# Order of transposes, weight loads and weight sums in the MLP block products of a two-layer decoder trunk

## The chip, the cores and the metric

One core of one Trainium2 chip runs the whole kernel in one launch. The metric is the time of one execution on the device, in microseconds (us). TensorE (PE in the profile; its weight loads are PEld) multiplies, VectorE (DVE), ScalarE (ACT) and GpSimd (POOL) do the elementwise work, and SyncE (SP) issues most of the loads from the chip's memory. Each engine works through a queue of its own; semaphores connect them.

## The reference, cut to what matters

A trunk of two layers over 256 tokens of width 2048. Each layer is a mixer (a recurrent one in layer 0, an attention in layer 1), a residual add, a norm, and then an MLP with a hidden width of 8192:

```python
def squared_relu_mlp(h, w1, w2):
    return jnp.square(jax.nn.relu(h @ w1)) @ w2
...
        h = h + squared_relu_mlp(rms_norm(h, norm_mlp[layer]), mlp_w1[layer], mlp_w2[layer])
```

All inputs and weights are float32. The change concerns the two MLPs, which take about two thirds of the time.

## The kernel before, in words

**Float32 from a faster type.** A weight tile of 128 x 2048 float32 numbers (1 MB) is loaded by SP and then split: ScalarE casts it into `hi` (L102, the type fp32r), and VectorE subtracts, `lo = w - hi` (L103). Activations are kept as such pairs too (`bufa`, `bufb`, `formx`, `formh`). Each product is three matmuls: high by high, high by low, low by high. One 1 MB tile holds four contraction blocks of 128 by 512 columns, so a use of it with one token half is 4 x 3 = 12 matmuls of 512 columns.

**Blocks.** An MLP is done in four quarters `q` of the hidden width. A quarter has four blocks of four 512-column groups taken two by two: `first` for n0 = 0 and 2 (w1, result into `bufb` and `formh`), then `second` for n0 = 0 and 2 (w2, result added to `xres`, which the profile calls `xall`). So there are 32 blocks in the kernel: 2 layers x 4 quarters x 4. A block covers 1024 columns (two groups, n = 0 and 1) and both token halves (j = 0 and 1). Half of its contraction goes by a scheme of seven products instead of eight, on sums of weights and sums of activations; the other half is plain. `blocks` runs over eleven steps, the *units*, in the order of `ORDERS`; `i0 + k` below is the number of the weight tile:

| step | weight it multiplies | matmuls |
| --- | --- | --- |
| a | tile 0 | 12 |
| t1 | tile 0 + tile 4 | 12 |
| n | tile 6 (w1) or 7 (w2), plain, both token halves | 24 |
| t2 | tile 0 + 4 + 5 | 12 |
| c | tile 5 | 12 |
| n | tile 7 (w1) or 6 (w2), plain | 24 |
| t3 | tile 4 + tile 5 | 12 |
| d | tile 1 | 12 |
| n | tile 2, plain (called n2 below) | 24 |
| t4 | tile 0 + 4 + 5 + 1 | 12 |
| n | tile 3, plain (called n3 below) | 24 |

The steps called n6 and n7 are the plain ones with tiles 6 and 7. All TensorE instructions of `mm` (L176) and `turn` (L179) are chained by hand in program order; the other engines' orders are set by the scheduler, which follows the program's order and two priorities: `stream()` for loads, sums and splits, and `urgent()` for what empties the accumulators.

**Weights.** `fetch` runs two units ahead of the multiplication and calls `combine` for a block's unit. Raw tiles come from the pool `wraw`, a ring of three buffers (tile name `raw`), and each split goes into rings of three `hi` and three `lo` buffers. So the split of a unit waits until TensorE has finished the unit three before it. The tiles `a` and `t1` are different: each has one buffer in the pool `pair` (the profile calls `t1` `t`). `a` is loaded there, split for step a, and then changed in place: at step t1 VectorE adds `t1` to it (L142), at step t2 it adds the raw tile 5, and at step t4, in w2, the raw tile 1. In w1 that last sum is made by a load that GpSimd issues and that adds in memory (L138). Tile 5 is added to `t1` by such a load in both (L136). In every step with a sum, VectorE's sum stands right ahead of the cast and the subtraction that split its result:

```python
        if add:
            V.tensor_tensor(r, r, held[add], OP.add)
        made[u] = Weights(r)
```

**Results and transposes.** `events` empties an accumulator after a product: in `first`, `hold` copies it (L710), and `final` combines it with such a copy on VectorE (L736); `relu2` then takes relu (L714) and square (L715) on ScalarE. When both token halves of a 512-column group are done, `to_h` appends a piece of work to the list `later`: eight transposes on TensorE into `pl` (L179), a cast (L690) and a subtraction (L691) into `bufb`, and for n < 2 also a copy (L694), four combinations (L592 to L595) and their splits (L588, L589) into `formh`. `flush` runs the list. In `blocks` it is called at the end of every plain step, after `final` of that step:

```python
            for j in (1, 0) if n else (0, 1):
                times(sums[n, j], w, lambda i, j=j, g=g: plain(j, 4 * g + i))
                if plains[n] == 2:
                    final(n, j, sums[n, j])
            flush()
```

In `second`, `to_x` (L745) adds the results to `xres`, and in the last quarter `done` appends `to_features`, the transposes for the next layer.

Of the kernel before, what the change touches and what calls it, by code (L numbers as in the profile page):

```python
# [10 lines left out]
F32 = mybir.dt.float32  # L11
# [5 lines left out]
OP = mybir.AluOpType  # L17
# [3 lines left out]
P = 128  # L21
# [20 lines left out]
def trunk_kernel(ctx, tc, x, xtok, cols, tab, masks, pos, fin, w_in, w_gate, w_out, w_qkv, w_o, w1, w2, out):  # L42
    nc = tc.nc
# [3 lines left out]
    wraw = pool("wraw", 3)  # L47
# [9 lines left out]
    V, A, T = nc.vector, nc.scalar, nc.tensor  # L57
# [7 lines left out]
    units = []  # L65
    made = {}
# [10 lines left out]
    for step in ORDER.split():  # L77
        src, first, n = where[step[0]]
# [29 lines left out]
    def fetch():  # L108
        u = at[0]
        if u >= len(units):  # L110
            return
        at[0] += 1
        src, i = units[u][:2]
        with stream():
            if len(units[u]) > 2:
                combine(u, *units[u])
                return
            r = wraw.tile([P, 2048], F32, name="raw")
            nc.sync.dma_start(r, src[i])
            made[u] = Weights(r, 1024)  # L120

    held = {}

    def combine(u, src, i, what, i0):
        if what in ("a", "t1"):
            r = held[what] = pair.tile([P, 2048], F32, name=what)
            nc.sync.dma_start(r, src[i])
        elif i is not None:
            r = wraw.tile([P, 2048], F32, name="raw")
            nc.sync.dma_start(r, src[i])  # L130
            held[what] = r
        to, add = {"t1": ("a", "t1"), "t2": ("a", "t2"), "t3": ("t1", "t2"), "t4": ("a", "d"),
                   "a": ("a", None), "c": ("t2", None), "d": ("d", None), "n": ("n", None)}[what]
        r = held[to]
        if what == "t2":
            nc.gpsimd.dma_start(held["t1"], src[i], accum_op=OP.add)  # L136
        if what == "c" and src in T4_DMA(w1, w2):
            nc.gpsimd.dma_start(held["a"], src[i0 + 1], accum_op=OP.add)  # L138
        if what == "t3" or what == "t4" and src in T4_DMA(w1, w2):
            add = None  # L140
        if add:
            V.tensor_tensor(r, r, held[add], OP.add)  # L142
        made[u] = Weights(r)

    def fetch_first():
        for u in range(4):
# [18 lines left out]
    def unit(src, i):  # L165
        u = at[1]
        assert units[u][0] is src and units[u][1] in (None, i), (u, i)
        at[1] += 1
        if u + 2 >= at[0]:
            fetch()  # L170
        return made.pop(u)
# [3 lines left out]
    def mm(*args, **kw):  # L175
        chain[:] = [after(T.matmul(*args, **kw), chain)]  # L176
# [3 lines left out]

    later = []

    def flush():
        todo = later[:]
        later.clear()
        for f in todo:
            f()

# [66 lines left out]
    class FirstNorm:  # L255
# [3 lines left out]
        def add(self, blk):  # L259
            self.n += 1  # L260
            q = wk.tile([P, S], F32, name="t1", bufs=2)
            A.activation(q, blk, AF.Square)
            if self.n == 1:
                self.ss.append(wk.tile([P, S], F32, name="q", bufs=1))
                V.tensor_copy(self.ss[0], q)
            elif self.n < KB:
                V.tensor_tensor(self.ss[0], self.ss[0], q, OP.add)
            else:
                self.ss.append(q)
# [49 lines left out]
    def tokens(src, i0, mov, kgs=(0, 1, 2, 3), by_k=False):  # L319
        ks = PAIRED if src is w2 else range(KB)  # L320
        ps = [pmm.tile([P, 512], F32, name="p") for _ in range(2)]
        for g in kgs:
            w = unit(src, i0 + g)
            order = [(j, i) for i in range(4) for j in range(2)] if by_k else \
                [(j, i) for j in range(2) for i in range(4)]
            for j, i in order:
                k = ks[4 * g + i]
                h, l = w.part(i * 512, 512)
                xh = mov[:, k, j * P:j * P + P]
                xl = mov[:, k, S + j * P:S + j * P + P]  # L330
                first, last = g == kgs[0] and i == 0, g == kgs[-1] and i == 3
                mm(ps[j], xh, h, start=first, stop=False)
                mm(ps[j], xh, l, start=False, stop=False)
                mm(ps[j], xl, h, start=False, stop=last)
            flush()
        return ps
# [9 lines left out]
    def project(src, i, mov, acc=None):  # L346
        w = unit(src, i)
        p = pmm.tile([P, 512], F32, name="p")
        jobs = [(k, mov[:, k], k == 0, k == KB - 1) for k in range(KB)]
        if later:  # L350
            cross(p, w, jobs[:8], "h")
            flush()
            cross(p, w, jobs[8:12], "h")
            cross(p, w, jobs[:12], "l")
            jobs = jobs[12:]
        (acc or cross)(p, w, jobs)
        return p
# [211 lines left out]
    for step in ORDER.split():  # L569
        i = int(step[1])  # L570
# [72 lines left out]
    def blocks(src, i0, n0, mov, forms, events, final):  # L643
        plain = lambda j, k: (mov[:, k, j * P:j * P + P], mov[:, k, S + j * P:S + j * P + P])
        form = lambda f, k: (forms[:, k, 0, f * P:f * P + P], forms[:, k, 1, f * P:f * P + P])
        side = {"a": lambda i: plain(0, 2 * i), "d": lambda i: plain(0, 2 * i + 1), "t4": lambda i: plain(1, 2 * i + 1),
                "t1": lambda i: form(3, i), "t2": lambda i: form(0, i), "t3": lambda i: form(1, i),
                "c": lambda i: form(2, i)}
        alpha, delta, gamma = (pmm.tile([P, 512], F32, name="p") for _ in range(3))
        beta = psc.tile([P, 512], F32, name="po" if n0 else "pd", bufs=1)  # L650
        bank = {"a": beta, "t1": alpha, "t2": beta, "c": alpha, "t3": beta, "d": gamma, "t4": beta}
        sums = {(0, 0): gamma, (0, 1): beta, (1, 0): alpha, (1, 1): delta}
        opened = []

        def times(bank, w, get):
            for i in range(4):
                h, l = w.part(i * 512, 512)
                xh, xl = get(i)
                mm(bank, xh, h, start=not any(b is bank for b in opened), stop=False, skip_group_check=True)
                opened.append(bank)  # L660
                mm(bank, xh, l, start=False, stop=False, skip_group_check=True)
                mm(bank, xl, h, start=False, stop=i == 3, skip_group_check=True)

        plains = [0, 0]
        for what, u in ORDERS[src is w2]:
            w = unit(src, None if u is None else i0 + 4 * n0 + u)
            if what != "n":
                times(bank[what], w, side[what])
                if what in events:
                    events[what](bank[what])  # L670
                continue
            n, g = divmod(u, 4)
            plains[n] += 1
            for j in (1, 0) if n else (0, 1):
                times(sums[n, j], w, lambda i, j=j, g=g: plain(j, 4 * g + i))
                if plains[n] == 2:
                    final(n, j, sums[n, j])
            flush()

    def to_h(n, tiles):  # L680
        def work():
# [21 lines left out]
    def first(i0, n0):  # L703
# [23 lines left out]
        def final(n, j, bank):  # L727
            with urgent():
# [5 lines left out]
                else:  # L734
                    y = keep["y2" if n else "y1"]
                    V.tensor_tensor(y, bank, y, OP.subtract if n else OP.add)  # L736
                    relu2(n, j, y, y)

        blocks(w1, i0, n0, bufa, formx, {"a": hold("y1", 2), "t1": hold("y4"), "t2": hold("y2"), "t3": u3}, final)

    def second(i0, n0, nrm, r2, r2n, done, gains):
        def to_x(bank, j, n, r, last):
            at = slice(n * 512, n * 512 + 512)
            with urgent():
                V.scalar_tensor_tensor(xres[:, j, at], bank, r[:, j:j + 1], xres[:, j, at], op0=OP.mult, op1=OP.add)  # L745
                if nrm and last:
                    nrm.add(j, n)

        def u2(bank):
            to_x(bank, 0, n0 + 1, r2n, False)  # L750
            if gains:
                gains()

        def u3(bank):
            to_x(bank, 1, n0 + 1, r2n, True)
            done(n0 + 1)

        blocks(w2, i0, n0, bufb, formh,
               {"a": lambda b: to_x(b, 0, n0, r2, False), "t1": lambda b: to_x(b, 1, n0 + 1, r2, False),
                "t2": u2, "t3": u3},  # L760
               lambda n, j, b: to_x(b, j, n0 + n, r2, (n, j) != (1, 1)))
        done(n0)
# [144 lines left out]
    with urgent():  # L907
        for j in range(2):
            m = tmp.tile([P, 1], F32, name="fm", bufs=2)
            r = tmp.tile([P, 1], F32, name="fr", bufs=2)  # L910
# [5 lines left out]
            i = V.scalar_tensor_tensor(m, ss[:, LAST:LAST + 1], 1.0 / D, m, op0=OP.mult, op1=OP.add)  # L916
            sums2.append(getattr(i, "ins", i).name)
            i = A.activation(t, m, AF.Sqrt)
# [6 lines left out]
        for j in range(2):  # L925
            for n, e in ((0, A), (LAST, V), (1, A if j else V), (3, V if j else A)):
# [4 lines left out]
                elif e is A:  # L931
                    i = A.activation(x_, x_, AF.Copy, scale=rr[j])
                    if n == 3:
                        after(i, roots[1:])
                else:
                    i = V.tensor_scalar(x_, x_, rr[j], None, op0=OP.mult)
# [19 lines left out]
T4_DMA = lambda w1, w2: (w1,)  # L956
# [104 lines left out]
```

## Time and profile before

Three runs took 2359.38, 2362.19 and 2363.51 us; the median is 2362.19 us.

| what | value |
| --- | --- |
| the profiled execution: time | 2363.19 us |
| its span, first to last instruction | 2361.0 us |
| mean granted TensorE clock | 0.971 |
| PE busy | 2201.3 us (93%), 11044 matmuls |
| PEld busy | 1864.1 us (79%) |
| DVE busy | 1788.7 us (76%) |
| ACT busy | 1265.5 us (54%) |
| POOL busy | 44.6 us (2%) |
| read from memory | 460.78 MB, 196 GB/s over the span |
| loads of `a` / `t1` by SP, 32 each: median to landing | 5.0 / 6.1 us |
| loads of `raw` for w1 and w2 by SP, 192: median to landing | 5.3 us |
| adding loads by GpSimd into `t1` (32) / `a` (16): median to landing | 7.8 / 8.5 us |

Busy shares are means over stages with different limits, and a matmul's end is modelled, so a busy PE is not a PE at its best rate. A row of a timeline gives start, duration, engine, line, operation, output and inputs, and in brackets the idle time before it with what ended it. A row of waits gives who waited for whom, the sum, the number and the longest in us. In windows, the columns are start and end, length, busy time of each engine with its number of instructions, the granted clock, the share of the DMA engines, and GB/s.

### The profile page before, as it was taken

The page shows a single profiled execution, that of the slowest core. Times are in us where ns is not written, and L with a number is a line of the kernel's source. Part 1 is how long each engine was busy: PE and PEld are TensorE (multiplying, and loading weights), DVE is VectorE, ACT ScalarE, POOL GpSimd, SP SyncE. Part 2 cuts the span into 40 slices and gives each one's busy share as a digit, 9 for nine tenths or more (in the row PEclk, how much of TensorE's full clock was granted, in tenths as well). Part 3 has the DMA queues.
Part 4 walks back from the last instruction along what each step waited for, and adds up shares of the span by engine and source line. Part 5 has one row for each costly group of instructions (what it writes and reads, how often), then busy time and mean ns, then how long its engine had stood idle before and what let it go on. Part 6 is the DMA issues. An engine that isn't in the chain of part 4 may idle for free.

```text
span 2361.0 us, 27739 instructions
## 1 busy us (share of the span) xinstructions
PE 2201.3 (93%) x11044; PEld 1864.1 (79%) x11044; DVE 1788.7 (76%) x2078; ACT 1265.5 (54%) x1429; POOL 44.6 (2%) x57
## 2 busy tenths in 40 slices
PE   9999999989989988989999999998998999899897
PEld 8999998767777777767788888887776777677776
DVE  7767786777777777777877878567777786777777
ACT  6444675564554565455554444556545545545644
POOL 0000000000000000000000000000000000000000
PEclk9999999989999999999999999999999999999999
DMA  8444465665765666665664554656667567566763
GB/s 306 150 164 156 143 219 191 196 198 176 249 219 173 196 213 214 214 214 178 199 212 161 179 179 161 214 170 202 217 214 214 178 221 242 179 191 212 237 216 107
DMA packets 65857, 464.68 MB, mean 197 GB/s; under 512 B 7344, under 2 KB 8112, under 8 KB 10304
## 3 DMA queue, kind: packets, MB, share of 16 engines
q1 hardware_dynamic: 58176, 410.89, 47.9%
q0 software_dynamic: 7264, 51.42, 11.6%
q8 instruction: 87, 1.43, 0.2%
q10 hardware_dynamic: 288, 0.61, 0.1%
q14 instruction: 42, 0.34, 0.0%
HBM read 460.78 MB, written 2.10 MB: 196 GB/s over the span
## 4 chain that ended last, share of the span: by engine, by line
PE 59%; DVE 16%; ACT 11%; DMA 7%; issue 6%; ACTq 0%; SPq 0%; DVEq 0%
PE p L176 47%; DVE lo L103 9%; ACT hi L102 9%; DMA a<-in_w 6%; DVE a L142 4%; PE pd L176 4%; PE po L176 4%; PE pl L179 2%; DMA raw<-in_w 1%; PE pl L471 1%; ACT y L714 1%; ACT y L715 1%; DVE xall L745 1%; DVE y L723 0%; DMA xall<-in_x 0%
## 5 line engine op out<-in xcount | busy, mean ns | idle before, releaser
L103 DVE TENSOR_TENSOR lo<-raw,hi 128x1024 fp32r<-128x1024 f32 (+2 forms) x454 | 748.4, 1667 | 195.5 <-ACT hi L102 178.5
L102 ACT CAST hi<-raw 128x1024 fp32r<-128x1024 f32 (+2 forms) x454 | 626.9, 1408 | 441.9 <-PE p L176 379.0
L176 PE MATMUL p<-hi,bufb 128*128 128x512 f32 x1408 | 448.3, 391 | 0.3
L103 DVE TENSOR_TENSOR lo<-a,hi 128x2048 fp32r<-128x2048 f32 x128 | 293.0, 2289 | 181.8 <-ACT hi L102 181.8
L102 ACT CAST hi<-a 128x2048 fp32r<-128x2048 f32 x128 | 244.3, 1908 | 328.8 <-DVE a L142 199.2
L176 PE MATMUL p<-hi,bufa 128*128 128x512 f32 x1280 | 411.0, 392 | 3.5 <-DVE bufa L231 2.7
L176 PE MATMUL p<-bufa,hi 128*128 128x256 f32 (+1 forms) x1792 | 364.9, 317 | 0.1
L176 PEld LDWEIGHTS p<-hi,bufb 128*128 128x128 f32 x1408 | 264.7, 188 | 57.0 <-DVE xall L745 2.4
L176 PEld LDWEIGHTS p<-bufa,hi 128*128 128x128 f32 x1792 | 294.5, 190 | 18.9 <-DVE hz L413 0.3
L176 PEld LDWEIGHTS p<-hi,bufa 128*128 128x128 f32 x1280 | 241.0, 188 | 54.8 <-DVE bufa L231 3.6
L176 PE MATMUL p<-lo,bufb 128*128 128x512 f32 x704 | 275.7, 392 | 6.2 <-DVE lo L103 6.2
L176 PE MATMUL p<-bufa,lo 128*128 128x256 f32 x1152 | 255.5, 287 | 0.0
L176 PE MATMUL p<-lo,bufa 128*128 128x512 f32 x640 | 251.1, 392 | 1.0 <-DVE lo L103 1.0
L176 PEld LDWEIGHTS p<-bufa,lo 128*128 128x128 f32 x1152 | 189.3, 191 | 2.7
L176 PEld LDWEIGHTS p<-lo,bufb 128*128 128x128 f32 x704 | 132.3, 188 | 37.5 <-DVE lo L103 10.8
L179 PE MATMUL pl<-tab__181,y 128*128 128x128 f32 x256 | 48.1, 350 | 106.4 <-ACT y L715 106.4
L176 PEld LDWEIGHTS p<-lo,bufa 128*128 128x128 f32 x640 | 120.6, 188 | 27.0 <-DVE lo L103 2.6
L179 PEld LDWEIGHTS pl<-tab__181,y 128*128 128x128 f32 x256 | 40.1, 182 | 115.2 <-ACT y L715 113.1
L142 DVE TENSOR_TENSOR a<-a,raw 128x2048 f32<-128x2048 f32 x48 | 109.6, 2283 | 0.0
L176 PE MATMUL po<-hi,bufa 128*128 128x512 f32 x256 | 94.4, 432 | 0.0
L176 PE MATMUL pd<-hi,bufb 128*128 128x512 f32 x256 | 91.7, 425 | 0.0
L176 PE MATMUL p<-hi,formh 128*128 128x512 f32 x256 | 87.2, 402 | 1.8 <-ACT hi L102 1.8
(281 smaller groups left out, 2891.7 us busy)
## 6 DMA issues: line engine op xcount, KB each, us to landing
raw<-in_w SPq DMA_DIRECT2D x192, 1024.0 KB, 5.3
raw<-in_w_qkv SPq DMA_DIRECT2D x48, 1024.0 KB, 4.8
raw<-in_w_in SPq DMA_DIRECT2D x46, 1024.0 KB, 4.9
a<-in_w SPq DMA_DIRECT2D x32, 1024.0 KB, 5.0
t<-in_w SPq DMA_DIRECT2D x32, 1024.0 KB, 6.1
t<-in_w POOLq DMA_DIRECT2D x32, 1024.0 KB, 7.8
raw<-in_w_out SPq DMA_DIRECT2D x16, 1024.0 KB, 4.9
a<-in_w POOLq DMA_DIRECT2D x16, 1024.0 KB, 8.5
```

The costliest lines, as they stand in the source:

```text
L102: A.copy(h, w)
L103: V.tensor_tensor(l, w, h.bitcast(F32), OP.subtract)
L142: V.tensor_tensor(r, r, held[add], OP.add)
L176: chain[:] = [after(T.matmul(*args, **kw), chain)]
L179: chain[:] = [after(T.transpose(out_, in_, ident), chain)]
L471: T.matmul(pl[:, j], kq[:, js], halves(qp[:, js], c, True), start=True, stop=True)
L714: A.activation(y, src, AF.Relu)
L715: A.activation(y, y, AF.Square)
L745: V.scalar_tensor_tensor(xres[:, j, at], bank, r[:, j:j + 1], xres[:, j, at], op0=OP.mult, op1=OP.add)
```

## The change

Three things are changed, all in the MLP blocks.

- `flush` takes a number `due`. `blocks` notes the length of `later` before the products of a plain step and runs only so many pieces after them, so what `final` appends in this step is run after the next plain step. What t3 of a block appends is run after n2 as before; what n3's `final` appends is run after the first plain step of the next block.
- Tile 0 (`a`) is loaded into the ring `wraw` instead of the pool `pair`. A new tile `s` in `pair` holds the sums, and the first one is written as `s = a + t1` instead of in place. The ring then takes seven tiles of a block instead of six.
- Each sum on VectorE is issued one step earlier: `a + t1` ahead of the split of a, the sum with tile 5 (and the load of tile 5 and GpSimd's adding load into `t1`) ahead of the split of the plain step before t2, and in w2 the sum with tile 1 ahead of the split of n2. In w1 GpSimd's adding load into the sum is issued after the split of c instead of ahead of it.

```diff
     def combine(u, src, i, what, i0):
-        if what in ("a", "t1"):
-            r = held[what] = pair.tile([P, 2048], F32, name=what)
-            nc.sync.dma_start(r, src[i])
-        elif i is not None:
-            r = wraw.tile([P, 2048], F32, name="raw")
-            nc.sync.dma_start(r, src[i])
-            held[what] = r
-        to, add = {"t1": ("a", "t1"), "t2": ("a", "t2"), "t3": ("t1", "t2"), "t4": ("a", "d"),
-                   "a": ("a", None), "c": ("t2", None), "d": ("d", None), "n": ("n", None)}[what]
-        r = held[to]
-        if what == "t2":
-            nc.gpsimd.dma_start(held["t1"], src[i], accum_op=OP.add)
+        def load(name, j, home=wraw):
+            held[name] = home.tile([P, 2048], F32, name="raw" if home is wraw else name)
+            nc.sync.dma_start(held[name], src[j])
+
+        def add(to, x, y):
+            V.tensor_tensor(held[to], held[x], held[y], OP.add)
+
+        if what == "a":
+            load("t1", i0 + 4, pair)
+            load("a", i)
+            held["s"] = pair.tile([P, 2048], F32, name="s")
+            add("s", "a", "t1")
+        elif what in ("n", "d"):
+            load(what, i)
+        ahead = units[u + 1][2:3] if u + 1 < len(units) else ()
+        if ahead == ("t2",):
+            load("c", i0 + 5)
+            nc.gpsimd.dma_start(held["t1"], src[i0 + 5], accum_op=OP.add)
+            add("s", "s", "c")
+        if ahead == ("t4",) and src not in T4_DMA(w1, w2):
+            add("s", "s", "d")
+        made[u] = Weights(held[{"t1": "s", "t2": "s", "t3": "t1", "t4": "s"}.get(what, what)])
         if what == "c" and src in T4_DMA(w1, w2):
-            nc.gpsimd.dma_start(held["a"], src[i0 + 1], accum_op=OP.add)
-        if what == "t3" or what == "t4" and src in T4_DMA(w1, w2):
-            add = None
-        if add:
-            V.tensor_tensor(r, r, held[add], OP.add)
-        made[u] = Weights(r)
+            nc.gpsimd.dma_start(held["s"], src[i0 + 1], accum_op=OP.add)
...
-    def flush():
-        todo = later[:]
-        later.clear()
+    def flush(due=None):
+        todo = later[:due]
+        del later[:due]
         for f in todo:
             f()
...
             plains[n] += 1
+            due = len(later)
             for j in (1, 0) if n else (0, 1):
                 times(sums[n, j], w, lambda i, j=j, g=g: plain(j, 4 * g + i))
                 if plains[n] == 2:
                     final(n, j, sums[n, j])
-            flush()
+            flush(due)
```

## The prediction

> **What bounds the kernel now.** I read the page's chain first, then TensorE's waits, then windows cut at the block borders, then the timeline of one border.
>
> ```profile
> PE 59%; DVE 16%; ACT 11%; DMA 7%; issue 6%; ACTq 0%; SPq 0%; DVEq 0%
> PE p L176 47%; DVE lo L103 9%; ACT hi L102 9%; DMA a<-in_w 6%; DVE a L142 4%; PE pd L176 4%; PE po L176 4%; PE pl L179 2%; DMA raw<-in_w 1%; PE pl L471 1%; ACT y L714 1%; ACT y L715 1%; DVE xall L745 1%; DVE y L723 0%; DMA xall<-in_x 0%
> ```
>
> TensorE carries 59%, but the load of `a`, the sums into `a` (L142) and the splits (L102, L103) sit on the chain too: at times weights come late. What TensorE itself waited for:
>
> ```profile
> PE pl L179 <- ACT y L715: 106.4, 16, 9.4
> PE p L176 <- DVE lo L103: 31.4, 24, 2.4
> PE p L176 <- ACT hi L102: 3.6, 6, 1.0
> ```
>
> Sixteen waits, 6.65 us each, stand before the transposes of `to_h`: one for each of the 16 `first` blocks. The windows of one quarter's four blocks (two `first`, two `second`; columns: length, busy TensorE, weight load, VectorE, ScalarE, GpSimd, then clock):
>
> ```profile
> 618.49:672.54 54.05, 44.12 (x197) 35.90 (x196) 42.01 (x28) 33.41 (x30) 2.59 (x3) 0.96 0.73 218
> 672.54:722.40 49.86, 44.77 (x199) 37.00 (x197) 37.46 (x30) 30.43 (x30) 1.73 (x2) 0.94 0.65 207
> 722.40:765.05 42.65, 42.65 (x182) 35.17 (x181) 30.57 (x21) 17.95 (x11) 0.00 (x0) 0.96 0.55 198
> 765.05:811.30 46.25, 43.05 (x181) 34.69 (x180) 37.56 (x23) 20.82 (x11) 0.86 (x1) 0.96 0.63 205
> ...
> sum 192.81, PE 174.59 PEld 142.76 DVE 147.60 ACT 102.60 POOL 5.18; mean PE 43.65 PEld 35.69 DVE 36.90 ACT 25.65 POOL 1.30
> ```
>
> The same arithmetic takes 42.65 us in one block and 54.05 in another. The end of the longest, on ScalarE and then on TensorE:
>
> ```profile
> 657.22 1.91 ACT L102 CAST hi<-a 128x2048 fp32r<-128x2048 f32 x1 [1.78 <-DMA a<-in_w]
> 659.03 0.57 ACT L694 COPY y<-pl 128x512 f32<-128x512 f32 x1
> 664.08 1.90 ACT L102 CAST hi<-a 128x2048 fp32r<-128x2048 f32 x1 [4.47 <-DVE a L142]
> 665.88 0.59 ACT L714 ACTIVATE y<-pd 128x512 f32<-128x512 f32 x1
> ...
> 669.72 1.15 ACT L715 ACTIVATE y<-y 128x512 f32<-128x512 f32 x2
> ```
> ```profile
> 662.54 0.39 PE L176 MATMUL pd<-hi,bufa 128*128 128x512 f32 x1
> 670.92 1.97 PE L179 MATMUL pl<-tab__181,y 128*128 128x128 f32 x8 [7.99 <-ACT y L715]
> ```
>
> TensorE finishes n3 at 662.9. The relu of that very block cannot start, because ScalarE's queue is held at the cast of the summed weight, which waits 4.47 us for the sum, which waited for the late `a`. So the last square ends at 670.9, then come the transposes. After such a gap the clock is halved for a while (first line right after the gap that ended at 477.96, second 20 us later):
>
> ```profile
> 478.00:482.00 4.00, 4.00 (x14) 3.51 (x15) 4.00 (x5) 1.17 (x2) 0.00 (x0) 0.50 0.83 291
> 500.00:504.00 4.00, 4.00 (x19) 3.30 (x19) 2.81 (x3) 0.48 (x2) 0.00 (x0) 1.00 1.00 406
> ```
>
> **The loss to be won.** The blocks span 426.5 to 1198.4 and 1581.1 to 2351.0: 771.9 + 769.9 = 1541.8 us. A block is 180 matmuls; undisturbed, 36 start in 8.16 us (chain pieces), 0.2267 us each, so 32 blocks need 1305.6. The 32 `to_h` take 0.79 us of TensorE each when warm (653.72 to 654.51), 25.3; five groups of feature transposes inside the stage, 4.0. Floor 1334.9; loss 206.9. It divides so: before the late transposes 106.4 idle; behind them the half clock, 1.62 instead of 0.79 us for the transposes and on average 1.50 us more than 10.88 for the next block's first 48 matmuls (sixteen borders), 16 x 2.33 = 37.3; the rest, 63.2, is late weights: 39.3 of listed idle time in some 40 waits, 23.9 of slower matmuls behind them and unlisted starts.
>
> One rule bears on the 37.3. The Trainium skill, page "TensorE: Matmul & The Clock Gate", section "What's actually happening", has the array fall to half clock after an idle window of about 3.4 us and recover after a busy one; by it, as an estimate, sixteen recoveries cost at least 16 x 1.7 = 27 us, so the gain would be some 10 us smaller, 2191 in the end; the trace's 0.50 agrees with the half clock, and its 37.3 decides.
>
> **The change, part by part.**
>
> *Transposes one step later.* `due` is taken before `final`, so only `to_h` of n3 moves: from the end of its block behind the first `n` product of the next one, 2.72 + 2.72 + 5.44 = 10.9 us of matmuls later. Eight transposes, two casts (0.59), two subtractions (0.68), and for half of them a copy, four combinations (0.42) and two split pairs (0.6 + 0.69) move with them. The square ended 8.0 us behind n3 at worst here (9.4 the longest wait), so it lies inside the 10.9 even if nothing else improved. Removed: 106.4 + 37.3 = 143.7. The user that could now be late is the `second` block with n0=0: its n7, then t2 and c (2 x 2.72 us), then n6, which reads the columns of the last `to_h`. Transposes end 0.8 us behind n7; two casts behind one weight cast (1.91) and two subtractions behind one sum and one split (2.28 + 2.29) end about 5.3 us behind them. That matches the 5.4 us to its use: at most 1 us in one block of four, 8 us over all.
>
> *`a` through the ring.* `a` had one buffer, read until the split of t4; the load left at 650.82, landed 6.4 us later, and the split followed at 657.22. Now `a` takes the slot of `d`, free when d is split, some 9 us earlier, so it lands before n3 is split. It hides behind t4 and n3 on TensorE (8.2 us). The price: seven ring loads per block instead of six on SP's one queue, so c is loaded into the slot of the preceding n3 instead of n2: one step later. Bytes and number of loads stay. The tile `s` takes the place of `a` in the pair pool.
>
> *Sums ahead of the split.* Eighty sums before, eighty after, 2.28 us each: VectorE's work is unchanged. But each now stands one step earlier, so ScalarE's cast no longer waits for it (those waits: 199.2 us in 45). In the built program's order on VectorE a border reads: split n3, a+t1, split a, split s, (a `first` result), s+c, split n6. Take 0 where TensorE ends n3. n3's cast waits for d's matmuls (13.6 us back in a `second` block), so its split ends at -9.3; a+t1 -7.0; split a, behind its cast (n2's end -8.2, +0.2, +1.9), -3.8; split s, behind its cast (t4's end -5.4), -1.0; one result 0.7, -0.3; s+c 2.0; another result 2.7; split n6 5.0. TensorE wants n6 at 5.44. Margin 0.4 us; the same sum through the `to_h` operations of a `first` border gives 5.6, late by 0.2. I count 0.5 us per block, 16 us. In w2 the sum s+d fits before n2's split, d having landed by 5.3 us after n6's split.
>
> *GpSimd's queue.* The accumulating load into t1 still waits for a+t1, 18 us and more before t3; the one into s (w1) still waits for the t2 split, 7.8 to 8.5 us to landing, with c, n7, t3, d and n2 (over 16 us) ahead of t4. Nothing is queued behind either. Costed at nothing; without that cover the longer landing, 8.5 us, would show.
>
> *The new wait.* s+c stands on VectorE ahead of the split of n6 and of everything behind it; if c has not landed, that whole queue, and then TensorE at n6, waits. c leaves at -9.3 and is wanted at -0.3: 9.0 us, against a landing of 5.3 (median) and 11.4 (longest for this tile). The bounds are 0 and 2.4 us per block (0 and 77 us in all). It is nearest to the median, as no accumulating load is in flight when c leaves: 0. But the accumulating load into t1 leaves 2.3 us behind it. A row for such a meeting, a chain piece 1.9 us behind an accumulating load:
>
> ```profile
> 1788.94 9.69 DMA raw<-in_w
> ```
>
> Landing so, c would be 0.7 us too late in each block, 22 us in all: 2203 instead of 2181; I keep the median, which is this tile's own. The Trainium skill, page "DMA: Bandwidth & Descriptors", section "Issuing engines are not separate DMA queues", says that transfers of all issuers interleave on the same 16 engines. That speaks against this edit and for the 2203; the row agrees with it.
>
> **Sum.** Against the profiled execution (2363.2; span 2361.0, so 2.2 around it; 1.0 over the median of 2362.2): 2363.2 - 206.9 + 16 (n6) + 5 (bufb for n6, of at most 8) + 3 (two entries of a layer, 1.36 and 1.35 us for bufa, untouched) = 2180.3; 2181 with 1 for tails.
>
> **Rivals.**
> - *VectorE becomes the bound.* Its 147.6 us in a quarter of about 167 is 88%; the densest stretch in my windows (1088 to 1181) had 83%. If in-order waits keep it there, a quarter takes 177.8, eight 1422.6: 2363.2 - (1541.8 - 1422.6) = 2244. For: the margins of 0.4 us. Against: its idle time now is mostly waiting for the casts that this change frees.
> - *Only the transposes help.* If the sums come no earlier in effect, TensorE meets the split of the summed weight next: at 662.9 + 2.7 it would want t1, whose low part ended at 668.3, 2.8 us. 2363.2 - 143.7 + 16 x 2.8 = 2264. Against: the built order has the sums ahead.
> - *Slower: c's load at the head of VectorE's queue.* It decides where c's landing exceeds 9.0 + 0.4 + 206.9/32 = about 16 us in every block; at 18 us each block waits 8.6, 32 x 8.6 = 275, so 2363 - 207 + 275 = 2431. For: c is now one slot later and the accumulating load follows it. Against: 11.4 is the longest landing. The Trainium skill, "TensorE: Matmul & The Clock Gate", section on the 16 sub-arrays, calls VectorE's queue strictly first in, first out, which this rival needs; the ScalarE hold at 664.08 shows such a hold.
> - *It does not do what it says.* If another edge still ties the relu's release to the border, 2363.
>
> **How the numbers follow.** Forecast case (2160 to 2205, c's 22 us inside) 0.65; VectorE bound (2205 to 2250) 0.17; transposes alone 0.06; unchanged 0.03; slower 0.04; better still, down to the floor of 2156, 0.05. The range 2156 to 2246 leaves out the three other rivals and the slowest VectorE cases, about 0.15. A measurement here tells 0.2% (about 5 us) from no change. Faster 0.93, same 0.03, slower 0.04.
>
> **What would show it.** Right: the sixteen waits of L179 on the square gone; clock 1.00 in the blocks; no load of `a` on the chain; VectorE near 88% in the stage; a quarter at 167 to 170 us; small waits at n6. Wrong: TensorE waits of over 1 us on `lo` at n6 with VectorE waiting for a ring load (c late), ScalarE waits on L130 sums (sums not ahead), or half clock still at the borders.

## The result, and the profile after

The changed kernel takes 2179.79 us (median of 4 runs, 2178.80 to 2180.80) against 2362.67 us before (4 runs): a ratio of 0.923, 95% interval 0.921 to 0.924. The profiled execution took 2178.80 us, with a span of 2177.0. The forecast was 2181.

The chain that ended last, from the page of the changed kernel (lines are some six higher than before: matmuls L181, transposes L184, sums L130, copies L716, relu and square L720 and L721):

```profile
PE 89%; ACT 5%; DVE 3%; issue 2%; DMA 1%; SPq 0%; DVEq 0%; ACTq 0%
PE p L181 63%; PE po L181 11%; PE pd L181 10%; ACT hi L102 3%; PE pl L184 2%; DVE lo L103 1%; PE pl L476 1%; DMA raw<-in_w 0%; ACT y L720 0%; ACT formh L593 0%; ACT y L716 0%; ACT y L721 0%; PE pl L864 0%; DMA xall<-in_x 0%; PE po L885 0%
```

TensorE's share of the chain went from 59% to 89%. The load of `a` (6%) and the sums (4%) are off it. What TensorE still waits for, from the waits of the changed kernel:

```profile
PE p L181 <- ACT y L716: 7.9, 8, 1.0
PE p L181 <- DVE lo L103: 2.9, 4, 1.0
PE p L181 <- DVE bufa L236: 2.7, 2, 1.4
PE p L181 <- DVE xall L751: 2.1, 2, 1.3
```

The 106.4 us before the transposes are gone, and the 31.4 us for low parts are 2.9. The same quarter in windows, block by block (length, busy TensorE, weight load, VectorE, ScalarE, GpSimd, clock, DMA share, GB/s):

```profile
596.90:638.61 41.71, 41.71 (x189) 34.62 (x188) 33.84 (x22) 26.58 (x22) 1.73 (x2) 1.00 0.84 256
638.61:682.49 43.88, 42.89 (x197) 35.37 (x196) 39.12 (x33) 30.61 (x31) 1.73 (x2) 1.00 0.79 236
682.49:724.18 41.69, 41.69 (x189) 34.62 (x188) 37.25 (x24) 23.87 (x17) 0.86 (x1) 1.00 0.70 227
724.18:765.30 41.12, 41.10 (x181) 33.72 (x180) 36.73 (x23) 21.09 (x11) 0.86 (x1) 1.00 0.71 230
sum 168.40, PE 167.39 PEld 138.34 DVE 146.94 ACT 102.15 POOL 5.18; mean PE 41.85 PEld 34.58 DVE 36.73 ACT 25.54 POOL 1.30
```

The quarter fell from 192.81 to 168.40 us with the same work on every engine (VectorE 147.60 then, 146.94 now). The clock is 1.00 in all four. One block stands out, 43.88 us: the second `first` block, with 0.99 us without a matmul. The stage spans 425.9 to 1106.8 and 1489.6 to 2167.1, 1358.4 us; before it was 1541.8, so it gives 183.4 of the 184.4 us between the two profiled executions.

### The profile page after: what moved, and what is told of

Read it like the earlier page. It is cut to its first block, busy times and chain, and to the rows that moved or that the text cites. A ratio compares the mean times of both kernels' runs of the same rounds, so it can differ in the third digit from the quotient of the medians.

```text
span 2177.0 us, 27718 instructions
## 1 busy us (share of the span) xinstructions
PE 2148.7 (99%) x11044; PEld 1834.7 (84%) x11044; DVE 1783.6 (82%) x2078; ACT 1261.1 (58%) x1429; POOL 44.6 (2%) x57
## 4 chain that ended last, share of the span: by engine, by line
PE 89%; ACT 5%; DVE 3%; issue 2%; DMA 1%; SPq 0%; DVEq 0%; ACTq 0%
PE p L181 63%; PE po L181 11%; PE pd L181 10%; ACT hi L102 3%; PE pl L184 2%; DVE lo L103 1%; PE pl L476 1%; DMA raw<-in_w 0%; ACT y L720 0%; ACT formh L593 0%; ACT y L716 0%; ACT y L721 0%; PE pl L864 0%; DMA xall<-in_x 0%; PE po L885 0%
## 5 line engine op out<-in xcount | busy, mean ns | idle before, releaser
L102 ACT CAST hi<-raw 128x1024 fp32r<-128x1024 f32 (+2 forms) x486 | 689.2, 1443 | 571.4 <-PE p L181 403.1
L103 DVE TENSOR_TENSOR lo<-raw,hi 128x1024 fp32r<-128x1024 f32 (+2 forms) x486 | 822.3, 1709 | 237.7 <-ACT hi L102 219.3
L181 PE MATMUL p<-hi,bufb 128*128 128x512 f32 x1408 | 448.5, 390 | 2.2 <-DVE xall L751 2.1
L181 PE MATMUL p<-hi,bufa 128*128 128x512 f32 x1280 | 412.5, 392 | 11.3 <-ACT y L716 7.9
L181 PE MATMUL p<-bufa,hi 128*128 128x256 f32 (+1 forms) x1792 | 364.9, 317 | 0.1
L181 PEld LDWEIGHTS p<-hi,bufb 128*128 128x128 f32 x1408 | 264.3, 188 | 60.0 <-DVE xall L751 5.6
L181 PEld LDWEIGHTS p<-bufa,hi 128*128 128x128 f32 x1792 | 294.5, 190 | 18.9 <-DVE hz L418 0.3
L181 PEld LDWEIGHTS p<-hi,bufa 128*128 128x128 f32 x1280 | 240.4, 188 | 65.5 <-ACT y L716 11.3
L181 PE MATMUL p<-lo,bufb 128*128 128x512 f32 x704 | 274.1, 389 | 1.0 <-DVE lo L103 1.0
L181 PE MATMUL p<-bufa,lo 128*128 128x256 f32 x1152 | 255.5, 287 | 0.0
L181 PE MATMUL p<-lo,bufa 128*128 128x512 f32 x640 | 250.5, 391 | 1.9 <-DVE lo L103 1.9
L103 DVE TENSOR_TENSOR lo<-s,hi 128x2048 fp32r<-128x2048 f32 x96 | 219.5, 2287 | 23.2 <-ACT hi L102 21.3
L102 ACT CAST hi<-s 128x2048 fp32r<-128x2048 f32 x96 | 183.7, 1913 | 48.1 <-PE po L181 21.7
L181 PEld LDWEIGHTS p<-bufa,lo 128*128 128x128 f32 x1152 | 189.3, 191 | 2.7
L181 PEld LDWEIGHTS p<-lo,bufb 128*128 128x128 f32 x704 | 132.2, 188 | 28.3 <-DVE lo L103 1.4
L181 PEld LDWEIGHTS p<-lo,bufa 128*128 128x128 f32 x640 | 120.4, 188 | 27.1 <-DVE lo L103 3.2
L130 DVE TENSOR_TENSOR s<-s,raw 128x2048 f32<-128x2048 f32 x48 | 109.6, 2284 | 1.7 <-DMA raw<-in_w 1.7
L181 PE MATMUL pd<-hi,bufa 128*128 128x512 f32 x256 | 84.8, 392 | 0.0
L181 PE MATMUL po<-hi,bufa 128*128 128x512 f32 x256 | 84.8, 392 | 0.0
L181 PE MATMUL p<-hi,formx 128*128 128x512 f32 x256 | 84.0, 389 | 0.0
L181 PE MATMUL p<-hi,formh 128*128 128x512 f32 x256 | 84.0, 389 | 0.0
L103 DVE TENSOR_TENSOR lo<-t,hi 128x2048 fp32r<-128x2048 f32 x32 | 73.2, 2287 | 12.4 <-ACT hi L102 12.4
```

Of the source, the lines that this page charges most:

```text
L102: A.copy(h, w)
L103: V.tensor_tensor(l, w, h.bitcast(F32), OP.subtract)
L130: V.tensor_tensor(held[to], held[x], held[y], OP.add)
```

## The experiments

Four kernels take the change apart; they ran beside the kernel before at 2359.97 us. Differences to the changed kernel below are to its 2179.79; the kernel before lay between 2359.0 and 2362.7 in the several sets of runs, so they are good to some 3 us.

**1. The later transposes alone** (on the kernel before):

```diff
-            flush()
+            flush(due)
```

> The kernel before with the later transposes alone: a, its in-place sums and their order stay. Theory A (the late transposes cost 143.7 us of their own and no more): 2363 - 144 = 2219. Theory B (the border is held by the late sum too, so TensorE meets the split of the summed weight next, 2.8 us at each of 16 borders, as in the rival of the prediction): about 2264, with TensorE waits on the low parts of L103 of over 2 us at the first borders, and no waits of the transposes on the square.

Measured: 2312.48 us (ratio 0.980, 0.977 to 0.983), a gain of only 50 us from the 2362.67 of the result, 47 from the kernel before beside it. Both theories are refuted, B less badly. TensorE's waits in it:

```profile
PE p L176 <- DVE lo L103: 61.9, 45, 2.4
PE p L176 <- ACT y L711: 20.7, 8, 3.2
PE p L176 <- ACT hi L102: 5.9, 10, 1.5
PE p L176 <- DVE bufb L692: 5.0, 8, 0.7
```

With the transposes out of the way, TensorE met the late weights: the waits for low parts doubled, 31.4 to 61.9 us, 45 instead of 24, and 20.7 us for a copy of an accumulator (L711) are new. While the transposes stood at the border, part of that lateness had passed unseen beside them.

**2. The weights alone** (the changed kernel with `flush()` instead of `flush(due)`):

> The changed kernel with the transposes where they were (right after the products of n3). Theory A (additive: 63 us of late weights won, the border's waits as before): 2179 + 144 = 2323. Theory B (the relu was held mainly by the late sum, so with the sums ahead the square ends about 4.2 us behind n3 instead of 8, and half clock follows): 16 x (4.2 + 2.3) = 104, so about 2283, with 16 waits of the transposes on the square of some 4 us each and a clock below 1 in the blocks.

Measured: 2260.91 us (0.958, 0.955 to 0.961), 102 us less than the 2362.67 (99 than the kernel before beside it): theory B, and still 22 us better than it. From its waits:

```profile
PE pl L184 <- ACT y L721: 48.1, 16, 3.0
PE pl L184 <- DVE y L600: 12.3, 8, 1.7
```

The same 16 waits for the square are 3.0 us long instead of 6.65, and the second line, 1.5 us each at half the borders, is new; 60 us instead of 106. So nearly half of what the profile of before booked under "transposes wait for the square" was the late weight, which held ScalarE's queue in front of the relu. The mean clock is 0.984: the half clock behind the border is not gone either.

**3. Each sum at the step that uses it:**

```diff
+        elif what == "t1":
+            held["s"] = pair.tile([P, 2048], F32, name="s")
+            add("s", "a", "t1")
+        elif what == "t2":
+            load("c", i0 + 5)
+            nc.gpsimd.dma_start(held["t1"], src[i0 + 5], accum_op=OP.add)
+            add("s", "s", "c")
+        elif what == "t4" and src not in T4_DMA(w1, w2):
+            add("s", "s", "d")
```

(the lines that issued them a step earlier are taken out).

> The changed kernel (later transposes, a through the ring, tile s) with each sum, the load of tile 5 and the adding load back at the step that uses them, right ahead of their split. If the sums ahead matter, ScalarE's casts wait for them again (199 us of waits before) and each block loses 0.5 to 1.5 us: 2195 to 2227. If the early load of a is what counted: within 5 us of 2179.

Measured: 2179.25 us, the time of the changed kernel. The two traces say why: the instructions of every engine stand in the same order, tile numbers aside. With a tile of its own for the sum and its inputs there early, the scheduler puts it ahead without these lines. The lines that move the sums up did nothing here.

**4. `a` in its one buffer again, summed in place** (transposes late, sums with tiles 5 and 1 ahead):

```diff
-            load("a", i)
-            held["s"] = pair.tile([P, 2048], F32, name="s")
-            add("s", "a", "t1")
+            load("a", i, pair)
+            held["s"] = held["a"]
+        elif what == "t1":
+            add("s", "a", "t1")
```

> The changed kernel with a back in its one buffer of the pair pool, summed in place, so a + t1 stands behind the split of a at step t1; the sums with tiles 5 and 1 stay ahead, and the transposes late. If the late load of a is what makes weights late, a leaves again only after the split of t4, the casts wait for its landing, and 1 to 2 us per block return: 2211 to 2243. If the load of a was hidden anyway: within 5 us of 2179.

Measured: 2314.70 us (0.981, 0.978 to 0.984): 135 us more than the changed kernel, the time of experiment 1. All that the weights bring comes from `a` in the ring together with `s`; the expectation was at most half of it. Experiments 8 to 10 take this apart.

**5. Tile 5 loaded twice**, to price the new wait at the head of VectorE's queue:

```diff
             load("c", i0 + 5)
+            nc.sync.dma_start(held["c"], src[i0 + 5])
```

> The changed kernel with tile 5 (step c) loaded twice into the same buffer, the second load waiting for the first, 1 MB more per block. By the border worked out in the prediction tile 5 is wanted 9.0 us after its load leaves (9.6 in the profile of the changed kernel); two loads in a row take some 10.4, so VectorE's queue waits 0.8 to 1.4 us at its head and TensorE 0.4 to 1.0 at n6: 13 to 32 us more, 2192 to 2211. If the wait at the head of VectorE's queue costs its whole length in each block: up to 2224. If there is more cover than worked out: within 5 us of 2179.

Measured: 2289.87 us (0.970, 0.967 to 0.972), 110 us more, twice the highest expectation. VectorE's timeline at a border, and its and TensorE's waits:

```profile
610.77 0.75 DVE L752 SCALAR_TENSOR_TENSOR xall<-po,nm,xall 128x512 f32<-128x512 f32 x1 [0.49 <-PE po L182]
614.66 2.29 DVE L130 TENSOR_TENSOR s<-s,raw 128x2048 f32<-128x2048 f32 x1 [3.13 <-DMA raw<-in_w]
616.87 2.28 DVE L103 TENSOR_TENSOR lo<-raw,hi 128x2048 fp32r<-128x2048 f32 x1
```
```profile
DVE s L130 <- DMA raw<-in_w: 101.6, 31, 5.9
...
PE p L182 <- DVE lo L103: 84.4, 32, 4.3
```

The split of n6 was ready behind the sum and could not pass it. The first load left at 601.44, the second at 606.27, and its data were there at 614.6: 8.4 us instead of the 5 of a usual load. The adding load into t1 (issued by GpSimd at 604.14) was in flight, and the next plain load left 0.6 us behind it. The changed kernel's trace tells the two apart: 30 of its plain loads of w1 and w2 shared over 4 us with an adding load and under 1 us with another plain one, and took 7.5 to 9.6 us (median 8.1); 59 that met next to no other such load took 4.9 (median). So the adding load is enough. In experiment 5 tile 5 came 13.2 us after its first load left, not 10.4. VectorE waited 3.3 us a block, TensorE 2.6, and slower matmuls behind such gaps (mean clock 0.984) make it 3.4. The slower rival of the prediction is real as a mechanism: a landing of 13 us takes back 60% of the gain. In the changed kernel itself the landing is short enough: VectorE waited for a tile in three sums, 1.7 us in all.

**6. The first sum done twice:**

```diff
             add("s", "a", "t1")
+            add("s", "a", "t1")
```

> The changed kernel with the sum a + t1 done twice in each block (same result), 32 more sums of 2.28 us on VectorE, 73 us in all. If VectorE is the bound (the rival): all 73 us show, 2252. If TensorE is, only what runs over the margin at the border shows: the split of n6 ends 5.9 us behind the border by the prediction's chain instead of 5.44, 0.5 us a block or more with the to_h operations: 2187 to 2203.

Measured: 2207.78 us (0.935, 0.932 to 0.937): 28 us for 73 us of VectorE work, a little over the range that goes with TensorE as the bound. A quarter of it:

```profile
600.91:774.10 173.19, 170.12 (x760) 139.27 (x759) 156.51 (x105) 103.73 (x81) 5.18 (x6) 1.00 0.74 233
```

VectorE is busy for 156.51 of 173.19 us, 90%. So it can be packed well above the 83% at which the rival held it; but more than a third of the added work shows, so the cover is thin. TensorE's waits for low parts are 14.6 us here, 2.9 in the changed kernel, and 5.6 us for `bufb` are new.

**7. The copy of the t1 product ahead of the cast of tile 5** (on the changed kernel; it answers the eight waits for L716):

```diff
     def hold(name, bufs=1):
...
-                    A.copy(keep[name], bank)
+                    i = A.copy(keep[name], bank)
+                    if name == "y4":
+                        copied.append(getattr(i, "ins", i).name)
...
         def split(self, at, n):
...
-            A.copy(h, w)
+            i = A.copy(h, w)
+            if copied:
+                after(i, [copied.pop()])
```

> The changed kernel with one edge more: on ScalarE the copy of the t1 product (tile y4) is ordered ahead of the cast of tile 5. The profile of the changed kernel has 8 waits of 0.99 us of TensorE for this copy, in the second half of n6, and a slower matmul behind each. If that is all they are: 8 x 1.1 = 9 us less, about 2170. If the cast of tile 5, now later, makes c late instead: no change or a little slower, 2178 to 2185.

What it goes for, on ScalarE of the changed kernel, and on TensorE:

```profile
644.95 1.92 ACT L102 CAST hi<-raw 128x2048 fp32r<-128x2048 f32 x1
646.75 0.63 ACT L593 CAST formh<-y 128x512 fp32r<-128x512 f32 x1
647.27 0.60 ACT L716 COPY y<-p 128x512 f32<-128x512 f32 x1
```
```profile
646.54 0.39 PE L181 MATMUL p<-hi,bufa 128*128 128x512 f32 x1
647.92 0.50 PE L181 MATMUL p<-hi,bufa 128*128 128x512 f32 x1 [0.99 <-ACT y L716]
```

The second half of n6 adds to the accumulator of t1, so it must wait until t1's product has been copied out; the copy stood behind a weight cast and a `formh` cast. Measured: 2169.32 us (4 runs, 2168.58 to 2170.02; 0.919, 0.917 to 0.921), 10.5 us less than the changed kernel, against 9 expected; the two intervals of the ratio do not meet. The eight waits are gone from the profile. It is the fastest version here.

**8. `a` early, but its first sum behind its split:**

```diff
-            add("s", "a", "t1")
...
+        if what == "a":
+            after(add("s", "a", "t1"), [made[u].last])
```

(`last` is the name of the split's subtraction.)

> The changed kernel with one edge more: on VectorE the first sum a + t1 is ordered behind the split of a, as an in-place sum has to be; a still comes early through the ring. As built, VectorE then does split a, a + t1, split of the sum, split n6, sum with tile 5, split t2. If the order of the first sum is a large part of what the separate tile s brings: the chain cast a, split a, sum, cast, split at the border is some 2 us longer and each block loses 1 to 2 us, 2211 to 2243. If the early load of a is nearly all of it: 2179 to 2195.

Measured: 2232.66 us (0.946, 0.941 to 0.951), 53 us more: 1.65 us per block, as the first theory said. ScalarE's waits for sums are back, and TensorE's for low parts:

```profile
ACT hi L102 <- DVE s L131: 185.2, 54, 6.0
PE p L183 <- DVE lo L103: 35.6, 28, 2.7
```

**9. `a` late, but its sum free:**

```diff
-            load("a", i)
+            r = load("a", i)
+            for n in t4_last:
+                tc.add_manual_dep(getattr(r, "ins", r), n, SYNC, reason="late")
```

(`t4_last` holds the subtraction of the last t4; the wait is a true semaphore wait on SP.)

> The changed kernel with the load of a made to wait for the split of the preceding t4, as its one buffer made it wait before; the tile s and the sums ahead stay. If the late load is most of the 133 us that separate the kernel with late transposes alone (2312) from the changed one: 2250 to 2312. By the border of the prediction (a lands some 5 us before the border, the sum, the splits and n6 follow 1.4 us late): about 2215, with waits at n6 on the low part. If the load was hidden anyway: within 5 us of 2179.

Measured: 2193.85 us (0.930, 0.926 to 0.934), 14 us more. The load now leaves at 629.87 and VectorE's sum waits for it only 0.31 us at this border:

```profile
635.02 2.29 DVE L132 TENSOR_TENSOR s<-raw,t 128x2048 f32<-128x2048 f32 x1 [0.31 <-DMA raw<-in_w]
```

This border is one of the mildest. Over the kernel VectorE waited for a landing ahead of 21 sums, 39.1 us in all and most often 2 to 3 us each; TensorE's waits for low parts rose from 2.9 to 12.0 us. So the load does come late, but most of that is covered ahead of TensorE, and it is not what cost most. The time lies between the second and the third expectation.

**10. Both edges at once:**

> The changed kernel with both edges at once: the load of a waits for the split of the preceding t4, and the first sum stands behind the split of a; the tile s stays a tile of its own, so nothing is summed in place. Alone the two cost 15 us (2194) and 53 us (2233) over 2179. If they add: 2247. If they are the two halves of what one buffer summed in place does, and are late one behind the other: about 2314, as the kernel with a in place, with half clock in the blocks again. Between the two: summing in place has a further cost of its own.

Measured: 2284.38 us (0.968, 0.964 to 0.972), 105 us more, between the two theories: 53 + 14 = 67 by themselves, and 38 more together. About 18 of the 38 are waits of TensorE for the copy of t1's product: 25.4 us in eight waits of up to 3.2 us, where each edge alone left 7.6. Behind the first of these eight (TensorE idle until 483.09) the matmuls started 0.43 us apart for about 3 us, so half clock is part of it too (mean clock 0.992). Why the copy is so late is not shown; presumably the sum now stands behind a split that is itself late, and ScalarE's queue is held with it. The remaining 30 us up to experiment 4 belong to summing in place beyond these two edges; which part of it was not tried.

## Why the prediction was right, and where its steps were not

**The total.** The floor of 1334.9 us for the stage was the step that carried the forecast, and it held: the blocks came to 1358.4, a rest of 23.5 where 24 to 25 was put. What that rest is made of was partly wrong (n6 below). The clock rose from 0.971 to 0.999 once no wait in the blocks was over 1.4 us, as the weighing of the half clock assumed.

**The division of the gain was wrong.** The prediction gave the transposes 143.7 us and the weights 63.2, by whom TensorE was waiting for in each gap. The runs give about 50 us for the transposes alone and 100 for the weights alone; done last, each gives 81 (2260.91 to 2179.79) and 133 (2312.48 to 2179.79). The step that failed is the one that added up idle time by its last releaser. The chain in the timeline of before already said otherwise: the square was late because the cast of the late sum held ScalarE. The prediction told that, and then booked the whole gap on the transposes. For the same reason its rival "only the transposes help" (2264) was 48 us too good: it priced one late split at 16 borders (44.8 us), and the run had 61.9 us of waits for low parts at 45 places, 20.7 for the copy and 5.9 for high parts.

**Sums ahead of the split.** The effect is there: ScalarE's 199.2 us of waits for the sums are down to 1.2. The cause was put in the wrong edit. Experiment 3 shows that the lines which issue the sums earlier change no instruction's place on VectorE or ScalarE; the tile `s` and the early `a` free the sum, and the scheduler moves it. Experiments 8 and 9 size the two, each lost alone: the order of the first sum 53 us, the early load 14; experiment 10 shows that together they are worth more than their sum.

**`a` through the ring.** Right that it would land in time and that c, one slot later, would too: 9.6 us from leaving (628.85) to use (638.46), against 9.0 worked out. The alternative of 2203 did not come: VectorE waited 1.7 us in all for tiles. The row that spoke for 2203 was of a load that left behind an adding one; tile 5 leaves 2.7 us ahead of it, and in the 32 blocks landed 4.7 to 6.2 us after leaving (median 4.9). The 11.4 us that the prediction called the longest landing of this tile is the longest of all loads named `raw`; tile 5's own took 4.7 to 7.7 in the profile of before, so the wait could have been put at nothing with more confidence. In the other order, in experiment 5, the load that met the adding one took 8.4 us instead of 5. The Trainium skill, page "DMA: Bandwidth & Descriptors", section "Issuing engines are not separate DMA queues", has all issuers' transfers interleave on the same engines; the trace agrees, with these 8.4 us.

**n6.** Predicted: ready 5.0 to 5.6 us behind the border, 16 us lost in all. Measured at 638.61: the split ran from 641.33 to 643.61, ready 5.0 us behind it, and TensorE did not wait there; in all the blocks it waited for a low part once, 0.96 us (until 1068.68). The 5 us for `bufb` did not show either. In their place came a wait that the prediction did not have: the copy of t1's product, 8 times, worth 10.5 us by experiment 7. It had traced what each split waits for, but not what an accumulator's second use waits for. So the 16 and 5 us put for n6 and `bufb` were not there. Of the 23.5, TensorE stood without a matmul for 13.8 us (1358.40 less 1344.64 busy; waits for the copy are 7.9 of it), and the other 9.7 are busy time above the floor. That the rest came out right is in part luck.

**Rivals.** VectorE as the bound: refuted by the 87% in the quarter above (146.94 of 168.40) and the 90% of experiment 6. The slower one: the mechanism exists, but a usual landing is 5 us and 9.6 are there. To lose the whole gain, 183 / 32 = 5.7 us a block, the landing would have to be about 15.5 us, an estimate from the 3.4 us lost at 13.2 if each further us costs one; 16 was put.

## What to carry to other kernels

Idle time booked to a releaser is not the gain of removing that releaser: where two late chains meet at one border, taking one away uncovers the other, so work out the floor of the stage for the total and test the parts alone. A value that is updated in place ties its next load and its next update to its slowest reader; here a tile of its own for the sum, with the early load that this allows, was worth 135 us, and moving the sums by hand nothing on top, as the scheduler had already done it. After such a change look for what now ends last: here it was one accumulator's copy, standing two casts too far back in ScalarE's queue, for another 10.5 us.

## What the runs showed of the hardware that was not expected

Gaps of 2 to 3 us can bring the half clock, but not each time. In experiment 5 a wait of 2.08 us (TensorE idle until 478.82) and one of 2.80 us (619.21) were each followed by matmuls started 0.43 us apart for about 3.4 us; waits of 2.46 us (665.25), 2.81 us (757.29) and 3.00 us (937.90) were followed by the usual 0.23. The granted clock was 0.50 from 619.20 to 622.60 and 1.00 from 757.20 to 760.60. In the blocks of the changed kernel, where the waits were 0.7 to 1.4 us long, none brought it.

A plain load of 1 MB that runs beside an adding load of GpSimd takes 8.1 us (median of 30 in the changed kernel) instead of 4.9, and a chain of two loads, the second beside such an adding load, cost 13.2 us in experiment 5, not twice one. The order matters: a plain load that left 2.7 us ahead of the adding one landed after 4.9 us (median of 32).
